# Up projection of a ConvFFN by seven block products instead of eight, with w_down and a gate by blocks of tokens

## The chip, the cores and the metric

One core of a Trainium2 chip. The metric is the device time of one execution in microseconds. Matmuls run on TensorE (PE), whose weight loads are shown as PEld; elementwise work on VectorE (DVE), ScalarE (ACT) and GpSimd (POOL); DMAs are issued from SyncE (SP).

## The reference

One inference step of a one-layer encoder over 1152 tokens (1024 of a prompt, 8 x 16 of samples), model width 1024, all in float32. The mixers (sparse attention, gated DeltaNet) and their merge come first, then what the change touches:

```python
x = x + mix @ w_out
h2 = rmsnorm(x, norm_ffn)
u_gate, u_val = split(h2 @ w_up, [D_FF], axis=-1)          # 1024 -> 2 x 2816
ext_f = concat([ffn_buf, u_gate], axis=1)
act = gelu(causal_dwconv(ext_f, conv_ffn), approximate=True)   # width 3
x = x + (act * u_val) @ w_down                             # 2816 -> 1024
gate_p = sigmoid(rmsnorm(x, norm_ple) @ w_ple_gate)        # 1024 -> 1024
x = x + gate_p * (p @ w_ple)
y = rmsnorm(x, norm_final)
```

## The kernel before, in words

Activations lie transposed: 128 features on the partitions, tokens along the free dimension. A dense product is a list of jobs (`_Job`, L245), each one weight tile of up to 8 x 128 rows and 128 output features. `weights` (L294) loads the tile ("wr"), casts it on ACT to a rounded part "wh" and subtracts on POOL (on DVE for jobs marked `late`) to get the rest "wl"; two pairs of wh and wl exist, so a tile is made while the two before it are used. `dense` (L345) runs a job's matmuls: for each of three blocks of 384 tokens and each k, three products of 128 x 128 by 128 x 384 into one PSUM bank (wh x H, wh x L, wl x H, where H and L are the activations' rounded part and rest), and an `evac` generator takes the bank from there. Three banks go round.

The order of all instructions is fixed ahead by a planner (`_Driver`, L75): each piece of work is a generator that asks for an engine or an event, and the piece that can start first by a table of costs goes next; `pick` (L1792) chooses between DVE and POOL by which is free first in that plan. Each engine then works through its list in that order, and so does SP with the DMAs.

The stages after the mixers are in `merge_ffn` (L2499). w_out (8 jobs) is evacuated by `evac_res` (L2309): add the residual x, store it (x2T), and make H2 and L2 of x times the norm's weight; the sum of squares goes along, and `rms` (L2357) makes the row R2 of reciprocal roots from it, by small matmuls and a Newton iteration of 11 small DVE instructions. The up projection is 44 jobs (`job_gate`, `job_val`, L2178, L2182), gate and value tile of one f in turn. `evac_gate` (L2364) multiplies by R2 into "fe", convolves on DVE into "fc", applies the gelu on ACT and multiplies by R2 again on POOL; `evac_val` (L2416) multiplies with the value product and splits the result into aH and aL, which stay in SBUF. So the FFN runs in four parts of 6, 6, 5 and 5 f: after each part w_down's 8 jobs over that part's rows run for all tokens, and their result is added to the residual through DRAM (x2T, x3T). The embedding's gate (w_ple_gate) runs for blocks 0 and 1 with one set of weights and then, weights loaded again, for block 2; `evac_pg` (L2458) applies it and `final` (L2484) the last norm.

```python
                    nc.tensor.matmul(acc, wh[:, kw], H, start=k == 0, stop=False)
                    nc.tensor.matmul(acc, wh[:, kw], L, start=False, stop=False)
                    nc.tensor.matmul(acc, wl[:, kw], H, start=False, stop=k == j.nk - 1)
```

Of the kernel before, what the change touches and what calls it, by code (L numbers as in the profile page):

```python
# [19 lines left out]
T = 1152  # L20
# [26 lines left out]
class _Banks:  # L47
# [16 lines left out]
    def give(self, t, at):  # L64
        self.free.append((at, self.held.pop(id(t))[1]))

# [178 lines left out]
class _Job:  # L245

    def __init__(self, src, nk, rhs, evac, m=128, blocks=range(NB), need=None, pre=None, late=0,
                 lag=False, spans=None):
# [6 lines left out]
        self.spans = spans or [slice(b * BW, b * BW + BW) for b in range(NB)]  # L255


class _Kernel:
# [34 lines left out]

    def weights(self):  # L294
# [4 lines left out]
        def fetch(j):  # L299
            wp, n = (self.wp2, "wr2") if j.late == 2 else (self.wp, "wr")  # L300
            j.raw = wp.tile([128, 8, 128], F32, name=n, bufs=1)[:, :j.nw, :j.m]
            nc.sync.dma_start(j.raw if len(j.evacs) == 1 else j.raw.rearrange("p (d k) c -> p d k c", k=j.nk), j.src)
        while True:
# [6 lines left out]
            if j.raw is not None and not j.late:  # L310
                yield j.loaded
            else:
                if j.raw is None:
                    yield SP
                    fetch(j)
                yield DMA
            nxt = next((x for x in self.jobs[i:] if x.src is not None), None)
            if j.late and nxt is not None:
                yield SP
                fetch(nxt)  # L320
            if len(used) > 1:
                yield used[-2].done
            wh = self.wp.tile([128, 8, 128], F32R, name="wh")[:, :j.nw, :j.m]
            yield ACT
            nc.scalar.copy(wh, j.raw)
            wl = self.wp.tile([128, 8, 128], F32R, name="wl")[:, :j.nw, :j.m]
            if j.late:
                yield DVE
                nc.vector.tensor_sub(wl, j.raw, wh.bitcast(F32))
            else:  # L330
                for k in range(0, j.nw, 2):
                    kk = slice(k, min(j.nw, k + 2))
                    yield POOL
                    nc.gpsimd.tensor_sub(wl[:, kk], j.raw[:, kk], wh[:, kk].bitcast(F32))
            j.w = wh, wl
            used.append(j)
            self.drv.set(j.prepared)
# [7 lines left out]
    def dense(self, jobs):  # L345
# [3 lines left out]
        for j in jobs:  # L349
            units = [(b, i, 0, j.nk) for i in range(len(j.evacs)) for b in j.blocks]  # L350
            if j.lag:
                units = [(b, 0, 0, j.nk - 1) for b in j.blocks] + [(b, 0, j.nk - 1, j.nk) for b in j.blocks]
            for b, i, k0, k1 in units:
                cols = j.spans[b]
                if k0 == 0:
# [10 lines left out]
                for k in range(k0, k1):  # L366
# [7 lines left out]
                    nc.tensor.matmul(acc, wh[:, kw], H, start=k == 0, stop=False)  # L374
                    nc.tensor.matmul(acc, wh[:, kw], L, start=False, stop=False)
                    nc.tensor.matmul(acc, wl[:, kw], H, start=False, stop=k == j.nk - 1)
                if k1 == j.nk:
                    if (b, i, k0, k1) == units[-1]:
                        drv.set(j.done)
                    drv.set(j.full[b])  # L380
        for e in ends:
            yield e

# [10 lines left out]
    def build(self):  # L394
# [5 lines left out]
        self.evs = _Banks(self.pool(ctx, "ev"), [128, BW], "evo", 4)  # L400
        self.accs = _Banks(self.pool(ctx, "psm", space=PSUM), [128, 512], "acc", 3, cols=BW)
# [20 lines left out]
        self.x3T = dp.tile([3, 8, 128, T], F32, name="x3T")  # L422
# [20 lines left out]
    def mixers(self):  # L443
# [37 lines left out]
        with ExitStack() as st:  # L481
# [6 lines left out]
            with ExitStack() as s2:  # L488
# [3 lines left out]
                drv.spawn(self.dense(jobs + self.jpp + self.jb), 9)  # L492
# [1636 lines left out]
    def merge_jobs(self):  # L2129
# [15 lines left out]
        self.jo = [_Job(I["w_out"][d], KD, two("MH", "ML"), self.evac_res(d, 0), pre=self.pre_load(lambda d=d: xT[d]),  # L2145
# [5 lines left out]
        self.A, self.C = {}, {}  # L2151
        self.aev = {f: [_Event() for _ in range(NB)] for f in range(22)}
        self.cev = {f: _Event() for f in range(22)}
        self.jf, f0 = [], 0
        for part, nf in enumerate((6, 6, 5, 5)):
            fs = list(range(f0, f0 + nf))
            if part == 0:
                self.jf.append(self.job_gate(fs[0]))
            for f in fs[1:] + [None]:
                if f is not None:  # L2160
                    self.jf.append(self.job_gate(f))
                elif part < 3:
                    self.jf.append(self.job_gate(f0 + nf))
                self.jf.append(self.job_val((f if f is not None else f0 + nf) - 1))
            src = (lambda d: self.x2T[d], lambda d: self.x3T[0][d], lambda d: self.x3T[1][d],
                   lambda d: self.x3T[2][d])[part]
            for d in range(8):
                self.jf.append(_Job(I["w_down"][d][:, f0:f0 + nf], nf,
                                    lambda k, cols, f0=f0: (self.A[f0 + k][0][:, cols], self.A[f0 + k][1][:, cols]),
                                    self.evac_res(d, part + 1), pre=self.pre_load(lambda d=d, src=src: src(d)),  # L2170
                                    need=lambda b, k, f0=f0: self.aev[f0 + k][b]))
            f0 += nf
        self.jp = [_Job(I["w_ple_gate"][d], KD, two("H3", "L3"), self.evac_pg(d), blocks=blocks,
                        pre=self.pre_ple(d), need=lambda b, k: self.rev[4][k][b],
                        late=(1 + d % 2) * (blocks == (2,))) for blocks in ((0, 1), (2,)) for d in range(8)]
        self.add_jobs(self.jpp + self.jb + self.ja + self.jo + self.jf + self.jp)

    def job_gate(self, f):  # L2178
        return _Job(self.I["w_up"][f], KD, lambda k, cols: (self.H2[:, k, cols], self.L2[:, k, cols]),
                    self.evac_gate(f), need=lambda b, k: self.rev[0][k][b])  # L2180

    def job_val(self, f):  # L2182
        return _Job(self.I["w_up"][22 + f], KD, lambda k, cols: (self.H2[:, k, cols], self.L2[:, k, cols]),
                    self.evac_val(f))
# [124 lines left out]
    def evac_res(self, d, step):  # L2309

        nc, drv = self.nc, self.drv

        def go(b, cols, acc, x):
# [3 lines left out]
            drv.give(self.accs, acc)  # L2317
            yield SP
            nc.sync.dma_start((self.x2T if step in (0, 4) else self.x3T[step - 1])[d][:, cols], x)
            if step in (0, 4):  # L2320
                H, L = (self.H2, self.L2) if step == 0 else (self.H3, self.L3)
                g = self.nrm[:, 1 if step == 0 else 2, d:d + 1]
                yield ACT
                nc.scalar.activation(H[:, d, cols], x, AF.Copy, scale=g)
                yield DVE
                nc.vector.scalar_tensor_tensor(L[:, d, cols], x, g, H[:, d, cols].bitcast(F32),
# [328 lines left out]
```

## Time and profile before

| | us |
|---|---|
| median of 3 runs | 2183.92 (2183.42 to 2184.28) |
| the profiled execution | 2187.6 |
| its span, first to last instruction | 2185.8 |
| busy: PE | 2117.6 (97%) |
| busy: DVE | 1227.8 (56%) |
| busy: POOL | 907.9 (42%) |
| busy: ACT | 847.9 (39%) |

The mean granted clock of TensorE was 0.988 of 2.4 GHz. Times of the trace count from the span's start. All instructions carry the line of one helper (L178), so they are told apart by their tiles: "acc" is a PSUM bank of a dense product, "rp" one of a norm.

### The profile page before, as it was taken

The numbers are of one execution on the slowest core, as the hardware profiler recorded it, in microseconds if no ns is written. First come the engines' busy times: TensorE is split into PE (matmuls) and PEld (weight loads), VectorE is DVE, ScalarE is ACT, GpSimd is POOL, SyncE is SP. The second block draws the span as 40 slices with busy tenths as digits, with TensorE's granted clock in tenths as the row PEclk, the third lists the DMA queues.
The fourth block names the chain that finished last, engine by engine and source line by source line (L and its number), as shares of the span: only waits on it lengthen the run. The fifth ranks groups of instructions, "written<-read, shape, count | busy, mean of one in ns | idle before, by whom it ended". The sixth has DMA issues, their size and how long they took to land.

```text
span 2185.8 us, 35741 instructions
## 1 busy us (share of the span) xinstructions
PE 2117.6 (97%) x12618; PEld 2061.5 (94%) x12618; DVE 1227.8 (56%) x3166; ACT 847.9 (39%) x1697; POOL 907.9 (42%) x1174
## 2 busy tenths in 40 slices
PE   7999988989999999999999999999999999999997
PEld 6898987989999889999999999999999999999997
DVE  7268988888757787774343444314441343244547
ACT  5266666566535556665133211101110111112432
POOL 5344433433234444454365445324442443343651
PEclk9999999989999999999999999999999999999998
DMA  5444366676655755457764311452135215413646
GB/s 192 121 119 102 79 179 160 157 200 178 178 171 161 217 161 170 141 163 230 235 203 143 90 40 40 91 168 46 47 65 172 64 40 128 134 40 97 193 155 202
DMA packets 326210, 298.99 MB, mean 137 GB/s; under 512 B 118332, under 2 KB 294032, under 8 KB 325904
## 3 DMA queue, kind: packets, MB, share of 16 engines
q1 hardware_dynamic: 326032, 296.71, 47.6%
q8 instruction: 100, 1.64, 0.4%
q14 instruction: 78, 0.64, 0.1%
HBM read 203.55 MB, written 94.71 MB: 136 GB/s over the span
## 4 chain that ended last, share of the span: by engine, by line
PE 62%; DMA 3%; DVE 1%; SPq 1%; issue 0%; POOL 0%; ACT 0%; DVEq 0%; ACTq 0%
PE acc L178 54%; PE at L178 7%; DMA evo<-gates 1%; PE rp L178 1%; DMA pbT<-evo 1%; SPq L178 1%; DMA r<-gsc 0%; DMA obT<-sg 0%; DMA sg<-sgb 0%; DVE evo L178 0%; DVE z L178 0%; POOL wl L178 0%; DVE X L178 0%; POOL tg L178 0%; DMA x<-qkv 0%
## 5 line engine op out<-in xcount | busy, mean ns | idle before, releaser
L178 PE MATMUL acc<-H,wh 128*128 128x384 f32 (+1 forms) x2592 | 897.2, 346 | 10.9 <-ACT wh L178 5.4
L178 PE MATMUL acc<-H,wl 128*128 128x384 f32 (+1 forms) x2592 | 876.9, 338 | 1.6 <-POOL wl L178 1.6
L178 PE MATMUL acc<-L,wh 128*128 128x384 f32 (+1 forms) x2592 | 876.5, 338 | 1.8 <-POOL L L178 1.3
L178 POOL TENSOR_TENSOR wl<-wr,wh 128x256 fp32r<-128x256 f32 (+1 forms) x572 | 484.2, 872 | 754.3 <-ACT wh L178 726.7
L178 PEld LDWEIGHTS acc<-H,wh 128*128 128x128 f32 x2592 | 488.9, 189 | 21.0 <-ACT wh L178 6.5
L178 PEld LDWEIGHTS acc<-L,wh 128*128 128x128 f32 x2592 | 489.1, 189 | 7.2 <-POOL L L178 2.0
L178 PEld LDWEIGHTS acc<-H,wl 128*128 128x128 f32 x2592 | 488.2, 188 | 4.3 <-POOL wl L178 2.9
L178 ACT CAST wh<-wr 128x1024 fp32r<-128x1024 f32 (+3 forms) x167 | 159.3, 954 | 580.3 <-PE acc L178 493.6
L178 DVE TENSOR_TENSOR xs<-xs,acc 128x384 f32<-128x384 f32 x120 | 66.5, 554 | 231.5 <-PE acc L178 146.0
L178 PE MATMUL acc<-aL,wh 128*128 128x384 f32 x528 | 178.0, 337 | 0.0
L178 PE MATMUL acc<-aH,wl 128*128 128x384 f32 x528 | 178.0, 337 | 0.0
L178 PE MATMUL acc<-aH,wh 128*128 128x384 f32 x528 | 178.0, 337 | 0.0
L178 DVE TENSOR_TENSOR fe<-acc,R 128x384 f32<-128x384 f32 (+1 forms) x88 | 38.2, 456 | 195.7 <-PE acc L178 195.7
L178 ACT ACTIVATE ja<-SC,cola 128x768 bf16<-128x768 f32 (+2 forms) x93 | 96.7, 1039 | 34.8 <-DVE cola L178 25.3
L178 PEld LDWEIGHTS acc<-aH,wl 128*128 128x128 f32 x528 | 99.0, 187 | 0.0
L178 PEld LDWEIGHTS acc<-aH,wh 128*128 128x128 f32 x528 | 99.0, 187 | 0.0
L178 PEld LDWEIGHTS acc<-aL,wh 128*128 128x128 f32 x528 | 99.0, 187 | 0.0
L178 POOL TENSOR_TENSOR ssq<-ssq,sqs 128x384 f32<-128x384 f32 x62 | 64.4, 1041 | 80.3 <-ACT sqs L178 80.0
L178 DVE SCALAR_TENSOR_TENSOR fc<-fe,cwf,fc 128x1024 f32<-128x1024 f32 (+1 forms) x88 | 95.0, 1080 | 3.1
L178 POOL TENSOR_TENSOR fc<-fc,R 128x288 f32<-128x288 f32 x88 | 75.0, 883 | 41.1 <-ACT fc L178 41.1
L178 DVE TENSOR_TENSOR sqs<-fc,acc 128x384 f32<-128x384 f32 x66 | 36.3, 550 | 79.7 <-PE acc L178 79.7
L178 ACT CAST aH<-sqs 128x384 fp32r<-128x384 f32 x66 | 33.8, 512 | 121.8 <-DVE sqs L178 121.8
(370 smaller groups left out, 3270.6 us busy)
## 6 DMA issues: line engine op xcount, KB each, us to landing
wr<-in_w_in SPq DMA_DIRECT2D x48, 512.0 KB, 3.7
wr<-in_w_up SPq DMA_DIRECT2D x44, 512.0 KB, 3.6
x3T<-xs SPq DMA_DIRECT2D x72, 192.0 KB, 1.9
xs<-x3T SPq DMA_DIRECT2D x72, 192.0 KB, 2.6
gates<-evo SPq DMA_DIRECT2D x48, 192.0 KB, 2.2
x2T<-xs SPq DMA_DIRECT2D x48, 192.0 KB, 2.0
xs<-x2T SPq DMA_DIRECT2D x48, 192.0 KB, 3.5
wr<-in_w_ple_gate SPq DMA_DIRECT2D x16, 512.0 KB, 3.5
```

Source lines behind the costliest of these rows:

```text
L178: r = f(*a, **k)
```

## The change

**Up projection.** For one f, the gate's weight tile is (a1, a2) and the value's (b1, b2), each half 4 x 128 rows of k; the input is cut into k halves and, in each block of 384 tokens, into a first and a second half of 192. That is a 2 x 2 by 2 x 2 block product, done by seven products (`_Up`, Strassen's scheme in Winograd's form) of 4 x 128 rows with 576 tokens, each in two PSUM banks of 288 columns (`up_products`). The weight sides are a1, a2, four sums of halves (`up_sums`: S1 = b1 + b2, S2 = S1 - a1, S3 = a1 - b1, S4 = a2 - S2) and b2; the token sides are two halves of the input and four sums T (`evac_out`, which takes the place of `evac_res` after w_out, and `up_parts`, which splits them). `evac_up` puts the products together with seven additions on DVE, `up_inner` convolves (first tap on ACT), applies the gelu and multiplies; the product goes to DRAM (AT). It is no longer multiplied by the norm's R2 on the value side: `evac_down` does that after w_down.

**w_down and gate.** For each block of 384 tokens: w_down with k in parts of 8, 8 and 6 tiles that accumulate in the same banks, output tiles 0 to 3 and then 4 to 7, followed by the 8 gate tiles. Every weight tile is loaded and split once per block. `load_up` brings a block's activations from DRAM and splits them; the residual is read from x2T straight into the result's buffer, and x3T goes. PSUM: three double banks (`ups`) in the up projection, the same as six single ones after it.

```diff
+A1X, A2X, S2T2, S3T3, S1T1, B2T4, S4Y = range(7)
...
+    def up_sums(self):
+        nc, q = self.nc, {}
+        for j in self.ju:
+            yield j.loaded
+            a1, a2, b1, b2 = j.raw
+            for n, i in enumerate((S1T1, S2T2, S3T3, S4Y)):
+                yield self.ju[j.f - 1].prepared[i] if j.f else self.hev2 if n < 2 else self.fev
+                o = q[n] = (self.hp if n < 2 else self.fp).tile([128, 4, 128], F32, name="s%d" % n, bufs=1)
+                x, y = ((b1, b2), (q[0], a1), (a1, b1), (q.get(1), a2))[n]
+                e, w = self.pick(DVE, POOL)
+                yield e
+                (w.tensor_sub if n else w.tensor_add)(o, x, y)
...
+    def up_rest(self, j, i, wh, wl):
+        e, q = self.pick(DVE, POOL) if j.f else (DVE, self.nc.vector)
+        n = 4 if e == DVE else 2
+        for k in range(0, 4, n):
+            yield e
+            q.tensor_sub(wl[:, k:k + n], j.parts[i][:, k:k + n], wh[:, k:k + n].bitcast(F32))
...
+    def up_products(self, j):
+        for i in range(7):
+            yield j.prepared[i]
+            wh, wl = j.w[i]
+            bank[i] = yield self.ups
...
+            for u in range(2):
+                acc = bank[i][:, u, :288]
+                for k in range(4):
+                    evs, H, L = self.up_rhs(i, u, k)
...
+                    nc.tensor.matmul(acc, wh[:, k], H, start=k == 0, stop=False)
+                    nc.tensor.matmul(acc, wh[:, k], L, start=False, stop=False)
+                    nc.tensor.matmul(acc, wl[:, k], H, start=False, stop=k == 3)
...
+        for b in range(NB):
+            for ds in (range(4), range(4, 8)):
+                heads = {}
+                for k0, k1 in ((0, 8), (8, 16), (16, 22)):
+                    for d in ds:
+                        j = _Job(I["w_down"][d][:, k0:k1], k1 - k0, up(k0), self.evac_down(d), blocks=(b,),
+                                 pre=self.pre_down(d), late=True, head=heads.get(d), last=k1 == 22,
+                                 need=lambda b, k, k0=k0: self.aev[k0 + k][b])
...
             for d in range(8):
...
+                self.jd.append(_Job(I["w_ple_gate"][d], KD, lambda k, cols, b=b: [x[:, k] for x in self.H3[b]],
+                                    self.evac_pg(d), blocks=(b,), pre=self.pre_ple(d), late=True,
+                                    need=lambda b, k: self.gev[k][b]))
...
+    def up_parts(self, t):
...
+        for k in range(4):
+            for b in range(NB):
+                yield self.opev[k][b]
+                yield self.tpev[4 + k][b]
+            R, H, L = self.TR[t][:, k], self.TH[t][:, k], self.TL[t][:, k]
+            yield ACT
+            nc.scalar.copy(H, R)
+            yield DVE
+            nc.vector.tensor_sub(L, R, H.bitcast(F32))
...
+    def evac_up(self, j, bank):
...
+        yield j.full[A1X]
+        yield ACT
+        nc.scalar.copy(u1, bank[A1X][:, :, :288])
...
+        yield from add(A2X, u3, u1)
+        yield from add(S2T2, u2, u1)
+        for e in self.Re[0]:
+            yield e
+        g, R = parts(ext[:, 2:2 + T]), parts(self.R2)
+        yield DVE
+        nc.vector.tensor_mul(g[:, 0], own(u3), R[:, 0])
+        yield from add(S3T3, u3, u2)
+        v = yield self.vs
+        vx, vy = [parts(v)[:, z] for z in range(2)]
+        yield from add(S1T1, vy, own(u3), OP.subtract, False)
+        yield from add(S1T1, u2, u2, OP.subtract)
+        yield from add(B2T4, vx, own(u3))
+        yield from add(S4Y, u2, u2, OP.subtract)
...
+    def load_up(self, b, fs):
+        for f in fs:
+            yield self.part_done[b - 1, f] if b else self.ju[21].done[(A1X, S2T2, S3T3, S1T1)[f // 6]]
+            yield self.ast[f]
...
+            nc.sync.dma_start(a, self.AT[f][:, b * BW:b * BW + BW])
+            yield DMA
+            yield ACT
+            nc.scalar.copy(H, a)
+            yield DVE
+            nc.vector.tensor_sub(L, a, H.bitcast(F32))
```

## Rows read from the trace of the kernel before

**Rows 1.** The page: the span and TensorE's share of it.

```profile
span 2185.8 us, 35741 instructions
...
PE 2117.6 (97%) x12618; PEld 2061.5 (94%) x12618; DVE 1227.8 (56%) x3166; ACT 847.9 (39%) x1697; POOL 907.9 (42%) x1174
```

**Rows 2.** Chain of waits: start us, us, engine, tile, instructions.

```profile
1133.33 92.48 PE acc L178 x532
...
1243.12 819.58 PE acc L178 x4707
...
2179.15 3.15 DVE X L178 x6
```

**Rows 3.** Windows: stretch, busy us of PE, PEld, DVE, ACT, POOL, clock, DMA.

```profile
1243.20:2062.60 819.40, 819.40 (x4709) 819.40 (x4707) 307.50 (x469) 152.80 (x211) 336.39 (x397) 1.00 0.34 88
1300.00:1400.00 100.00, 100.00 (x578) 100.00 (x578) 42.75 (x65) 18.44 (x24) 45.73 (x52) 1.00 0.23 44
2135.00:2169.00 34.00, 34.00 (x202) 34.00 (x202) 31.94 (x70) 13.28 (x21) 6.11 (x6) 1.00 0.77 252
```

**Rows 4.** Timeline of PE in w_out: start us, us, instruction.

```profile
1184.57 0.34 PE L178 MATMUL acc<-MH,wh 128*128 128x384 f32 x1
...
1185.09 0.34 PE L178 MATMUL acc<-MH,wh 128*128 128x384 f32 x1
```

**Rows 5.** Timeline, all engines, attention: 272 columns.

```profile
870.62 0.28 PE L178 MATMUL at<-skL,sbH 128*128 128x272 f32 x1
870.62 0.19 PEld L178 LDWEIGHTS at<-skH,sbH 128*128 128x128 f32 x1
...
870.74 0.29 PE L178 MATMUL at<-skH,sbH 128*128 128x272 f32 x1
...
870.99 0.34 PE L178 MATMUL acc<-H,wh 128*128 128x384 f32 x1
```

**Rows 6.** Timeline of PE in the input projection: 448 columns.

```profile
62.28 0.37 PE L178 MATMUL acc<-L,wh 128*128 128x448 f32 x1
...
63.11 0.37 PE L178 MATMUL acc<-H,wl 128*128 128x448 f32 x1
```

**Rows 7.** Lines by form, 1240 to 2060 us, DVE: busy us, mean ns.

```profile
L178 DVE SCALAR_TENSOR_TENSOR fc<-fe,cwf,fc 128x1024 f32<-128x1024 f32 x44 | 72.4, 1645 | 1.6
L178 DVE TENSOR_TENSOR xs<-xs,acc 128x384 f32<-128x384 f32 x94 | 52.1, 554 | 184.0 <-PE acc L178 113.6 <-DMA xs<-x3T 47.5 <-DMA xs<-x2T 20.1
L178 DVE TENSOR_TENSOR aL<-sqs,aH 128x384 fp32r<-128x384 f32 x66 | 51.0, 773 | 33.4 <-ACT aH L178 33.4
...
L178 DVE SCALAR_TENSOR_TENSOR fc<-fe,cwf,fc 128x128 f32<-128x128 f32 x44 | 22.7, 515 | 1.6
```

**Rows 8.** Lines by form, 1240 to 2060 us, POOL and ACT.

```profile
L178 POOL TENSOR_TENSOR wl<-wr,wh 128x256 fp32r<-128x256 f32 x251 | 232.0, 952 | 442.4 <-ACT wh L178 440.0 <-DMA out_cf<-fe 2.4
...
L178 ACT ACTIVATE H<-xs,nrm 128x384 fp32r<-128x384 f32 x22 | 13.5, 616 | 23.2 <-DVE xs L178 23.1
```

**Rows 9.** Timeline of DVE, around the norm and in the up projection.

```profile
1232.91 0.16 DVE L178 SCALAR_TENSOR_TENSOR rs_a<-rs_a,rr_m 128x3 f32<-128x3 f32 x1
...
1341.59 0.55 DVE L178 TENSOR_TENSOR aL<-sqs,aH 128x384 fp32r<-128x384 f32 x1
...
1344.66 1.05 DVE L178 TENSOR_TENSOR aL<-sqs,aH 128x384 fp32r<-128x384 f32 x1 [0.58 <-ACT aH L178]
```

**Rows 10.** Lines, 2136 to 2169 us (gate, last block), DVE and ACT.

```profile
L178 DVE TENSOR_TENSOR wl<-wr,wh 128x1024 fp32r<-128x1024 f32 x6 | 7.3, 1218 | 0.1
L178 ACT CAST wh<-wr 128x1024 fp32r<-128x1024 f32 x6 | 6.3, 1045 | 2.2 <-PE acc L178 2.2
```

**Rows 11.** The page: DMA packets, and issues (KB each, us to landing).

```profile
DMA packets 326210, 298.99 MB, mean 137 GB/s; under 512 B 118332, under 2 KB 294032, under 8 KB 325904
...
x2T<-xs SPq DMA_DIRECT2D x48, 192.0 KB, 2.0
xs<-x2T SPq DMA_DIRECT2D x48, 192.0 KB, 3.5
```

More of the change, by code (lines that the diff above doesn't have):

```diff
@@ L255, in __init__ @@
         self.spans = spans or [slice(b * BW, b * BW + BW) for b in range(NB)]
+        self.head, self.last = head or self, last
+class _Up:
+    src = 0
+    def __init__(self, f):
+        self.f, self.w = f, [None] * 7
+        self.prepared, self.done, self.full, self.summed = [[_Event() for _ in range(7)] for _ in range(4)]
+        self.loaded, self.parts = _Event(), {}
+A1X, A2X, S2T2, S3T3, S1T1, B2T4, S4Y = range(7)
 class _Kernel:
@@ L291, in split, with pair, part @@
         (self.nc.vector if eng == DVE else self.nc.gpsimd).tensor_sub(L, x, H.bitcast(F32))
+    def pair(self, used, k, c, m, ev):
+        if len(used) > 1:
+            yield used[-2]
+        used.append(ev)
+        return [self.wp.tile([128, 8, 128], F32R, name=n)[:, :k, :m] for n in ("wh", "wl")]
+    def part(self, wh, wl, raw):
+        nc = self.nc
+        yield ACT
+        nc.scalar.copy(wh, raw)
+        n = raw.shape[1]
+        for k in range(0, n, 2):
+            kk = slice(k, min(n, k + 2))
+            yield POOL
+            nc.gpsimd.tensor_sub(wl[:, kk], raw[:, kk], wh[:, kk].bitcast(F32))
     def weights(self):
@@ L316, in weights @@
                 yield DMA
[L317 to L323, printed above, removed]
-            yield ACT
[L325 to L334, printed above, removed]
@@ new lines, in landed, with down_weights @@
+    def landed(self, j, t):
+        self.drv.cur.dma = t
+        yield DMA
+        self.drv.set(j.loaded)
+    def down_weights(self, j, used):
+        n = len(self.down)
+        if n > 2:
+            yield self.down[-3]
+        else:
+            yield used[n - 2] if n < 2 else self.ju[21].done[B2T4]
+        self.down.append(j.done)
+        if n % 3 == 2:
+            t = self.TH[3].rearrange("p a b c -> p (a b c)")
+            wh, wl = [t[:, z:z + j.nw * 128].rearrange("p (k m) -> p k m", m=128) for z in (0, 1024)]
+        else:
+            wh, wl = [self.wp.tile([128, 8, 128], F32R, name=x)[:, :j.nw] for x in ("wh", "wl")]
+        yield j.loaded
+        yield ACT
+        self.nc.scalar.copy(wh, j.raw)
+        self.drv.spawn(self.down_rest(j, wh, wl), 1)
@@ new lines, in merge_ffn @@
+            for i in (1, 2):
+                self.ups.views[i] = p.tile([128, 2, 512], F32, name="up%d" % i)
+                self.ups.free.append((0.0, i))
+            self.accs = _Views([x[:, i, :BW] for x in self.ups.views for i in range(2)])
+            self.accs.free = []
+            ends = drv.spawn(self.dense(self.jd), 9, self.ju[21].done[S4Y])
+            drv.spawn(self.down_loads(), 1)
+            for i in range(4):
+                drv.spawn(self.load_up(0, range(i, 22, 4)), 1)
```

548 lines of the change are left out of this document (384 added, 164 removed).

## The prediction

> **What bounds the kernel now.** I read the page first. The span is 2185.8 us and TensorE (PE) is busy for 97% of it [rows 1]; the profiled execution took 2187.6 us, 3.7 us over the median of the three runs, 2183.92. The sum below is one of differences within that execution, and I lay it against the median.
>
> Then the chain of waits. From 1133 us to 2170 us it is matmul upon matmul: 92.48 us of the output projection, some 17 us with the norm's small matmuls and a few waits among them, then 819.58 us without a break [rows 2]. The windows say the same of that stretch: PE busy for 819.40 of 819.40 us, clock 1.00 (2.4 GHz), DVE busy for 38%, POOL 41%, and the DMA at 88 GB/s [rows 3]. The reader should see that in the ConvFFN nothing but PE counts: work taken from other engines there is worth nothing, and a matmul column saved is worth its full time as long as the others keep up. So the sum needs the price of a column, and the rest is whether the others keep up.
>
> **Matmuls: the gain.** Before, the up projection is 44 weight tiles x 3 token blocks x 8 k x 3 products = 3168 matmuls of 384 columns. After, it is 22 x 7 products x 2 halves x 4 k x 3 = 3696 matmuls of 288 columns: 7/8 of the columns in 7/6 of the instructions. No row has 288 columns, so I take the nearest sizes. Matmuls of 384 columns start (1185.09 - 1184.57) / 3 = 0.1733 us apart [rows 4]; 578 in 100 us gives 0.1730 [rows 3]. Those of 272 columns, each with weights of its own, start (870.99 - 870.62) / 3 = 0.1233 us apart [rows 5]; those of 448, (63.11 - 62.28) / 4 = 0.2075 us [rows 6]. Per column this is 0.451, 0.453 and 0.463 ns: in proportion, with no fixed part that can be seen. Between 272 and 384, 288 columns come to 0.1304 us. The stage goes from 3168 x 0.1733 = 549.0 us to 3696 x 0.1304 = 482.0 us: **-67.0 us**. The ends are 3/4 of 0.1733 (480.4 us, -68.6) and 288/448 of 0.2075 (493.0 us, -56.0). w_down (1584 matmuls) and the embedding's gate (576) keep count and size.
>
> A rule speaks against this. In the window the weight loads are busy for all of the time, just as the matmuls are [rows 3], and one takes 0.19 us [rows 5], more than the 0.1733 us between two matmuls. By the Trainium skill, "Perfetto Trace Analysis", Identifying the Most-Contended Engine, TensorE's headroom is to be judged by the busy share of LDWEIGHTS and not of the matmuls; by that this stage would be full of loads, and 528 more of them would make it longer. The trace bears it out as little as it can: in [rows 5] loads of 0.19 us follow each other at the matmuls' 0.12 us, so loads overlap and their share isn't the bound at 288 columns. It stays a rival.
>
> **The start of the up projection.** The first product needs only the rows of the first four output tiles; the second needs the last tile's third block through DVE (0.55, [rows 7]), ACT (0.62, [rows 8]) and twice DVE (some 1 us), about 2.5 us with handoffs, under a first product of 24 x 0.1304 = 3.1 us. The tight one is the sixth, which starts at 15.6 us and needs the third set of T operands; its last k is read some 1.2 us later. By then DVE has to do: the rest of the last evacuation 2.5; 12 splits of 576 columns; 4 weight splits of 512; 5 additions and products of 576; the reciprocal root, 11 x 0.16 [rows 9]. DVE's price by size comes from 550 ns for 384 columns (shortest, [rows 9]) and 1218 ns for 1024 [rows 10]: 0.149 us + 1.044 ns per column, so 0.75 for 576 and 0.68 for 512. The sum is 2.5 + 9.0 + 2.7 + 3.75 + 1.8 = 19.8 us against 16.8: **+3 us**, between 0 (the order hides it) and 6 (a few of these wait for POOL, below). Behind such a wait only PE's next products are queued. The norm's small matmuls are 9 + 9 as before.
>
> **The up projection, steady.** One f takes PE 168 x 0.1304 = 21.9 us. DVE now has, per f: 7 additions from PSUM of 576 columns, 5.25; the products with R, 0.75 + 1.2; the convolution, 4 x 512 and 2 x 128 columns, 5.0 (the groups of 1024 and 128, 1645 and 515 ns [rows 7], give 1.26 ns per column and 1.0 for 512); two products of 576, 1.5; together 13.7 us. Four sums and seven splits of 512 columns go to DVE or POOL, whichever the planner thinks free: with six on DVE 4.1, so 17.8 us of 21.9; POOL's five cost some 1.9 each (two of 256 at 952 ns, [rows 8]), 9.5 us. POOL's product with R is gone. ACT has seven casts of 512 columns, a copy of 576, three taps and the gelu of 1152 each, 6500 columns in all, which at 1045 ns for 1024 [rows 10] is 7 to 8 us. So no engine is over PE's time, but DVE is at 81% where it was at 38%, and DVE and POOL get into each other's way: a split of 384 columns takes 0.55 us alone and 1.05 when POOL works at the same time [rows 9], 773 ns on average [rows 7]. With the mean factor of 1.4 on the two-input work in SBUF that the group means do not already hold (1.95 + 1.5 + 4.1 = 7.55), DVE comes to 20.8 us. The PSUM ring holds three products, so an evacuation may be two products (6.3 us) late before PE notices; weights are made two products ahead. I take **+2 us** for the stage, between 0 and the rival below.
>
> **w_down and gate by blocks.** Every weight tile is loaded, cast and split for one block of 24 matmuls (4.2 us) and no longer for three. The trace shows this already: in its last 34 us the gate runs so, with a cast of 1045 ns and a split of 1218 ns per tile [rows 10], DVE at 94%, DMA at 252 GB/s, and PE busy for 34.00 of 34.00 us [rows 3]. The new stage asks for less of each: per tile a split in two halves (1.4), an activation's split 0.92 x 0.55 and a third of an evacuation (0.55 + 0.55 + 0.62), 2.5 of 4.2 us of DVE; and in 124.8 us per block (720 matmuls) 24.8 MB, which is 15.7 of weights, 4.3 of activations and 4.7 of residual, embedding and output: 198 GB/s. At the change from w_down to the gate the last tile goes DVE 0.55, DVE 0.55, ACT 0.62, DVE 0.6 and four handoffs, about 3.2 us, under 7 k of the first gate tile, 21 x 0.1733 = 3.6 us. Three such places, 0 to 1.5 us each: **+2 us** in all, from 0 to 5.
>
> **At nothing.** The activations' trip through DRAM: f = 21 needs some 10 us for its inner part, 2.0 and 3.5 us for store and load [rows 11] and 1 us for the split, some 17 us; the first matmul on it comes 8 tiles, 33 us, after the stage ends. The loads on SP wait for stores of f that were done one f earlier; behind a late one stand only later loads of the same kind, with four weight tiles already fetched. The x3T traffic (144 transfers) goes. The tail (last DVE work at 2179.15 [rows 2]) is unchanged.
>
> **Sum:** -67.0 + 3 + 2 + 2 = -60, so 2183.9 - 60 = **2124 us** (2128 for a profiled execution).
>
> **Rivals.** (a) DVE with POOL becomes the bound of the up projection. If each of the shared operations waits as long as the worst row (1.05 / 0.55 = 1.9), DVE needs 5.25 + 5.0 + 7.55 x 1.9 = 24.6 us per f, 2.7 over PE's, x 22 = 59 us, and the gain is gone. With the mean factor, nothing is lost. The middle gives 2153. For it: 1.4 to 1.9 is not far, and the order is fixed ahead by a planner. Against it: at 94% of DVE PE didn't wait [rows 3]. By the Trainium skill, "SBUF — State Buffer", Who interferes with whom, the pair of ports is an exclusive lock, which is how 0.55 becomes 1.05. Chance 0.15.
> (b) Slower: the weights of w_down and gate, loaded three times, set the pace through the DMA. If the queues carry no more than the kernel's mean of 137 GB/s [rows 11], a block takes 24.8 MB / 137 = 181 us for 125, +56 x 3 = 168, 2292 us. It cancels the gain at 67 us over three blocks, that is from about 170 GB/s down. Against it: 252 GB/s held for 34 us without a gap [rows 3]. Chance 0.05.
> (c) The change buys no PE time, as a matmul's pace is set by its weight load: 3696 x 0.1733 = 640.5, +91.5, with the +7 about 2282. Against it: [rows 5]. Chance 0.03.
>
> **Numbers.** Forecast 0.75, (a) 0.15, (b) 0.05, (c) 0.03, no difference for another reason 0.02. Faster by over 0.2% (4.4 us, about what can be told from no change) is the forecast and (a): 0.90; same 0.02; slower 0.08. The range goes from the largest gain without a stall (2183.9 - 68.6, and 2 us of waits around the norm that could go, 2113) to the middle of (a), 2153; that leaves out some 2 in 10.
>
> **What would show it.** Right: matmuls of 288 columns 0.130 us apart; the up stage near 482 us with PE at 100%, DVE near 80%; each block of w_down and gate near 125 us; clock 1.00. Wrong: PE idle repeatedly before S or T products (weights or operands from DVE and POOL: a); waits of the cast for w_down's DMA (b); 0.17 us between matmuls of 288 columns (c).

## The result, and the profile after

The changed kernel takes 2161.07 us (median of four runs, 2153.31 to 2164.95) against 2183.73: ratio 0.9892, 95% interval [0.9863, 0.9921]. In a second series of five runs it took 2160.96 against 2182.02, 0.9899 [0.9881, 0.9917]. It is faster by 21 to 23 us, where 60 were forecast, and the forecast's range (2113 to 2153) doesn't hold it.

The profiled execution took 2153.31 us. It is the shortest run of the changed kernel, and that of the old kernel, 2187.6, one of its longest, so the two spans differ by 34.3 us and not by 22. The table, read from the starts of PE's matmuls, says where:

| stretch | before, us | after, us | difference |
|---|---|---|---|
| to the first w_out matmul | 1127.6 | 1113.5 | -14.0 |
| w_out | 104.1 | 102.7 | -1.4 |
| last w_out matmul to the last of the gate | 937.6 | 917.8 | -19.8 |
| of which up projection (288 columns) | | 506.5 | |
| of which w_down and gate | | 411.0 | |
| behind it | 16.5 | 17.5 | +1.0 |

The first row is not the change's (shown below), and the last isn't either: behind the last gate matmul the profiles of both kernels show 16.5 us in some runs and 17.5 in others. Nor can 1.4 us be told in w_out, which took 102.1 to 105.2 us over the profiles of kernels that leave nothing out. The third row is the change's: it repeats to 0.5 us in either kernel (937.6 again in e2_before_ev_right, 917.3 to 917.8 in the changed kernel's other two), and it was forecast as -60. The page of the profile after:

```profile
span 2151.5 us, 37608 instructions
PE 2065.3 (96%) x13146; PEld 2005.0 (93%) x13146; DVE 1543.1 (72%) x3585; ACT 1001.0 (47%) x1979; POOL 838.2 (39%) x1028
```

PE lost 52 us of busy time against [rows 1], and DVE gained 315. The windows of the profile after, by stage (columns as in [rows 3]): the first block f = 0 of the up projection, the blocks after it, and w_down with the gate.

```profile
1216.40:1255.10 38.70, 32.57 (x205) 31.27 (x205) 27.48 (x46) 15.41 (x28) 13.37 (x13) 0.87 0.22 61
1255.10:1700.00 444.90, 444.90 (x3357) 444.90 (x3356) 366.67 (x470) 148.38 (x241) 255.53 (x249) 1.00 0.39 75
1723.00:2134.00 411.00, 391.24 (x2221) 382.53 (x2220) 262.58 (x477) 168.61 (x251) 45.17 (x41) 1.00 0.57 173
```

The middle line is what [rows 3] showed of the old kernel: PE never idle, clock 1.00, though DVE is now at 82%. The losses stand in the other two: 6 us idle and a granted clock of 0.87 in the first block, 20 us idle in the last stage. There the waits of PE are (us in total, times, longest):

```profile
PE up L192 <- DVE gt L192: 12.0, 15, 1.4
PE up L192 <- ACT wh L192: 3.0, 4, 0.7
PE up L192 <- ACT T3H L192: 2.2, 3, 0.7
PE up L192 <- DVE L L192: 1.4, 3, 0.6
PE up L192 <- DVE T2L L192: 0.9, 1, 0.9
PE up L192 <- ACT H L192: 0.2, 1, 0.2
```

`gt` is the tile into which DVE evacuates an accumulator. That is odd, for six accumulators go round and PE needs one every 4.2 us. The timeline of one such place, in the gate (start us, us; in brackets the engine's idle time and what ended it):

```profile
1836.50 0.34 PE L192 MATMUL up<-H,T3H 128*128 128x384 f32 x1
1836.67 0.34 PE L192 MATMUL up<-H,wh 128*128 128x384 f32 x1
...
1838.90 1.01 DVE L192 TENSOR_TENSOR gt<-up,R 128x384 f32<-128x384 f32 x2
...
1840.28 0.34 PE L192 MATMUL up<-H,wl 128*128 128x384 f32 x1
1840.66 0.56 DVE L192 TENSOR_TENSOR gt<-up,R 128x384 f32<-128x384 f32 x1 [0.75 <-PE up L192]
...
1841.27 0.44 PE L192 MATMUL up<-H,wh 128*128 128x384 f32 x1 [0.65 <-DVE gt L192]
1841.56 0.33 PE L192 MATMUL up<-L,wh 128*128 128x384 f32 x1
```

An output of the gate is 24 matmuls. The third ends with the matmul of 1836.50 (weights in `T3H`), the fourth begins at 1836.67 (weights in `wh`) and goes into another PSUM bank. DVE evacuates the first two outputs from 1838.90 on. Then it stands idle for 0.75 us before it takes the third, which has long been complete: it starts only when the fourth output's 18th matmul, of 1840.28, is over. And PE goes on with the 19th only when DVE is done, 0.99 us after the 18th instead of 0.17. So each engine waits for the other, though the two are at different banks. Every second output of the gate has this (1841.27, 1849.50, 1857.73), and two in four of w_down's third parts: 21 of the 26 pauses of over 0.6 us from start to start. The waits put down to ACT's weight copies are of this kind too, but for the first: at 1763.34, 1812.20 and four more places PE goes on 0.15 us after an evacuation's end. All that lies over the usual distance of the matmuls in this stage comes to 27.8 us.

### The profile page after: what moved, and what is told of

It is laid out like the page before. It is cut to its first block, busy times and chain, and to the rows that moved or that the text cites. A ratio compares the mean times of both kernels' runs of the same rounds, so it can differ in the third digit from the quotient of the medians.

```text
span 2151.5 us, 37608 instructions
## 1 busy us (share of the span) xinstructions
PE 2065.3 (96%) x13146; PEld 2005.0 (93%) x13146; DVE 1543.1 (72%) x3585; ACT 1001.0 (47%) x1979; POOL 838.2 (39%) x1028
## 4 chain that ended last, share of the span: by engine, by line
PE 56%; DVE 4%; DMA 4%; issue 1%; ACT 1%; POOL 1%; SPq 1%; DVEq 0%; ACTq 0%; POOLq 0%
PE up L192 38%; PE acc L192 12%; PE at L192 6%; PE rp L192 1%; SPq L192 1%; DVE B L192 1%; DVE gt L192 1%; DVE wl L192 1%; DMA evo<-gates 1%; DMA T<-in_w_down 0%; POOL tg L192 0%; POOL wl L192 0%; DVE z L192 0%; DMA obT<-sg 0%; DMA x<-qkv 0%
## 5 line engine op out<-in xcount | busy, mean ns | idle before, releaser
L192 PE MATMUL acc<-H,wh 128*128 128x384 f32 (+2 forms) x1344 | 475.6, 354 | 6.9 <-DVE evo L192 2.1
L192 PE MATMUL acc<-L,wh 128*128 128x384 f32 (+2 forms) x1344 | 456.6, 340 | 1.8 <-POOL L L192 1.3
L192 PE MATMUL acc<-H,wl 128*128 128x384 f32 (+2 forms) x1344 | 456.6, 340 | 1.4 <-POOL wl L192 1.4
L192 POOL TENSOR_TENSOR wl<-wr,wh 128x256 fp32r<-128x256 f32 (+1 forms) x288 | 232.5, 830 | 302.0 <-ACT wh L192 285.8
L192 PEld LDWEIGHTS acc<-H,wh 128*128 128x128 f32 (+1 forms) x1344 | 253.5, 189 | 15.8 <-DVE evo L192 2.4
L192 PEld LDWEIGHTS acc<-L,wh 128*128 128x128 f32 (+1 forms) x1344 | 253.8, 189 | 6.9 <-POOL L L192 2.0
L192 PEld LDWEIGHTS acc<-H,wl 128*128 128x128 f32 (+1 forms) x1344 | 253.4, 189 | 3.6 <-POOL wl L192 2.4
L192 PE MATMUL up<-B,wh 128*128 128x288 f32 x704 | 143.2, 297 | 3.5 <-DVE B L192 2.8
L192 DVE SCALAR_TENSOR_TENSOR T<-fe,cwf,T 128x512 f32<-128x512 f32 x132 | 124.6, 944 | 17.8 <-ACT T L192 16.4
L192 PE MATMUL up<-T,wh 128*128 128x288 f32 (+1 forms) x416 | 125.6, 302 | 2.2 <-DVE T L192 2.2
```

The lines of the kernel that those rows point to most:

```text
L192: r = f(*a, **k)
```

## The experiments

Times of stages are from each kernel's profile: "first block" from the first matmul of f = 0 to that of f = 1, "up" and "w_down, gate" from first to last matmul. The median is of all timed runs (one run where marked *).

| kernel | first w_out matmul | first block | up | w_down, gate | median |
|---|---|---|---|---|---|
| changed | 1113.5 | 38.7 | 506.5 | 411.0 | 2161.07 |
| changed, again (c_after_again) | 1117.8 | 38.7 | 506.5 | 410.5 | 2160.96 |
| e3_after_ev_left | 1121.0 | 38.7 | 506.4 | 410.9 | 2158.30 |
| e1_ring | 1120.0 | 38.7 | 506.4 | 394.7 | 2139.64 |
| e1b_ring_again | 1118.5 | 35.6 | 503.3 | 394.6 | 2139.67 |
| e10_six_tiles | 1113.9 | 38.7 | 506.4 | 392.3 | 2138.13 |
| e9_gate_pair | 1118.1 | 37.0 | 504.8 | 391.1 | 2137.95 |
| e6_256 (256 columns) | 1114.1 | 38.7 | 484.3 | 391.0 | 2111.53* |
| e4_ring_late_parts | 1119.7 | 40.0 | 507.7 | 395.2 | 2142.42 |
| e5_casts_first | 1126.0 | 40.5 | 508.2 | 392.6 | 2150.44* |
| e7_no_norm | 1113.2 | 36.3 | 504.5 | 395.1 | 2133.43* |
| e8_no_low | 1123.6 | 27.0 | 496.0 | 393.7 | 2133.12* |

### The pauses in w_down and the gate

The six accumulators are the two halves of three two-bank tiles, and successive outputs got half a and half b of the same tile. **e1_ring** changes their order alone (`_Ring` hands them out in strict rotation):

```diff
-self.accs = _Views([x[:, i, :BW] for x in self.ups.views for i in range(2)])
+self.accs = _Ring([x[:, i, :BW] for i in range(2) for x in self.ups.views])
...
-self.accs.free += [(self.drv.cur.t, i), (self.drv.cur.t, i + 1)]
+self.accs.free += [(self.drv.cur.t, i), (self.drv.cur.t, i + 3)]
```

> The changed kernel with another order of its six accumulators in w_down and the gate: successive outputs get halves of different two-bank tiles instead of the two halves of one. Every engine keeps its instructions and their order. Theory A (a matmul into one half of a tile waits for VectorE's read of the other half, and lets go about 0.15 us after that read ends): nearly all of the 26 pauses of about 1 us, 27.8 us together, go; from the first to the last matmul of w_down and the gate 411.0 us becomes 384 to 388, and the whole 20 to 27 us less. Theory B (the matmul waits for an accumulator that is really still in use, or for its weights): the pauses stay where they are, 411 us, and the whole changes by less than 3 us.

Measured: 394.7 us for the stage, 16.3 less, and a median of 2139.64 (0.9796 [0.9768, 0.9825] of the old kernel). That is short of theory A's 384 to 388, as nearly all was expected to go. Of the 21 pauses at an evacuation none stays where it was; but 11 pauses of over 0.6 us are there, and counted as the 27.8 us were, 11.7 us are left (the expectation of e9 counts 9 pauses with 9.7 us, by a narrower measure). The other five of the 26 stay, and six are new. Two of the six are of the old kind, at the gate's fourth output, which gets the other half of the tile of the first, and the first waits for the norm:

```profile
PE up L204 <- DVE gt L204: 1.4, 2, 0.7
```

But this moves two things at once: which tile an output belongs to, and which bank DVE reads while PE writes. **e10_six_tiles** parts them. It keeps the order and the banks, and closes the up projection's PSUM pools to declare six tiles of one bank each:

```diff
+for st, side, of in ((self.up1, None, (1, 2)), (self.up0, "right", (0,))):
+    if got >= set(of):
...
+        st.close()
+        p = self.pool(st, "dn%d" % of[0], space=PSUM, **({"side": side} if side else {}))
+        for i in range(2 * of[0], 2 * of[-1] + 2):
+            self.accs.views[i] = p.tile([128, 512], F32, name="dn%d" % i)[:, :BW]
...
```

> The changed kernel with its accumulators in the old order, successive outputs in neighbouring PSUM banks as before, but each bank declared as a tile of its own once the up projection is done with it. Instructions, order and banks stay; what can differ is only which waits the program's own bookkeeping puts on the matmuls. Theory A (the 1 us pauses are that bookkeeping's: a read of one half of a tile holds up writes to the other half): the pauses go as they did with the other order, w_down and the gate take 393 to 397 us instead of 411. Theory B (the chip itself holds a matmul back while VectorE reads the neighbouring bank): 409 to 412 us, and only another order of banks helps.

Measured: 392.3 us, 18.7 less than the changed kernel and just below theory A's 393; median 2138.13 (0.9822 [0.9797, 0.9846]). Its window and the waits of PE in it:

```profile
1723.40:2115.70 392.30, 386.90 (x2221) 383.46 (x2220) 262.08 (x477) 167.75 (x251) 49.73 (x41) 1.00 0.59 181
```

```profile
PE rp L192 <- POOL ssq L192: 1.5, 2, 0.8
PE dn L192 <- DVE L L192: 1.5, 3, 0.6
PE dn L192 <- ACT H L192: 1.1, 3, 0.6
PE dn L192 <- DVE T2L L192: 0.9, 1, 0.9
PE dn L192 <- ACT T3H L192: 0.3, 1, 0.3
```

Every engine has the instructions of the changed kernel in the same order (DVE 262 us in both windows), but no wait for `gt` is left, and one of 0.3 us for a weight copy. The place in the gate that answers to the one above, on PE, in the middle of the fourth output, and on DVE, which evacuates the first three outputs in one go:

```profile
1836.91 0.34 PE L192 MATMUL dn<-H,wl 128*128 128x384 f32 x1
1837.09 0.34 PE L192 MATMUL dn<-H,wh 128*128 128x384 f32 x1
1837.26 0.34 PE L192 MATMUL dn<-L,wh 128*128 128x384 f32 x1
1837.43 0.34 PE L192 MATMUL dn<-H,wl 128*128 128x384 f32 x1
```

```profile
1836.04 1.48 DVE L192 TENSOR_TENSOR gt<-dn,R 128x384 f32<-128x384 f32 x3
```

DVE reads the third output's bank to 1837.52 without having waited, and PE goes on in the neighbouring one at 0.173 us a matmul. (That the banks are those of the changed kernel follows from the edit; the profile doesn't number them.) So the chip doesn't hold the matmul back: the wait was in the program. Its bookkeeping of who reads and writes what goes by tiles: a read of half a had to wait for the writes to half b that stood ahead of it, and held up the next write to half b. (By the Trainium skill, "PSUM — Partial Sum Buffer", PSUM bank collisions raise a hardware error, a matmul's write and another engine's read at the same time raise an error in one bank and run clean in two different ones; the rows, with two banks, agree.)

**e9_gate_pair** goes for the pauses that are left. It is e1_ring with the gate's first two outputs of each block taken together, k = 0 to 6 of both, then k = 7 of both:

```diff
+for k0, k1 in ((0, 7), (7, 8)):
+    for j in (j0, j1):
...
+        for k in range(k0, k1):
+            yield j.need(b, k)
```

> As the kernel with the new order of accumulators; in each block of tokens the first two outputs of the gate take seven of their eight k first, both of them, and then the last k of both, so that TensorE has 3.6 us more work before it needs what w_down's last output leaves. Theory A (the pauses that are left in this stage, 9 of them with 9.7 us, are the three handovers from w_down to the gate: the last k waits for the last output's high and low part, 1.7 us, then the norm's matmul for GpSimd's sum, 1.1 us, and the third accumulator for an evacuation that waits for the norm, 1.1 us): 4 to 8 us of them go, 394.8 becomes 387 to 391. Theory B (the chain behind w_down's last output is longer than this cover, or the waits only move to the norm): 393 to 396.

Measured: 391.1 us, 3.6 less; 7.9 of the 11.7 us are left. The waits for w_down's last output are gone, and one of the two for the norm's sum; those for an evacuation behind the norm went from two with 1.4 us to three with 2.2. That is just short of theory A's 387 to 391; in the median (2137.95 against 2139.67) it can't be told.

### The start of the up projection

In the first block PE waits 6.1 us, and behind the waits the clock is low. The timeline of the changed kernel, DVE and POOL at the end of w_out (1216.2 us), then PE:

```profile
1214.70 0.41 DVE L192 SCALAR_TENSOR_TENSOR T<-xs,nrm,sqs 128x192 f32<-128x192 f32 x1
1217.30 1.08 DVE L192 TENSOR_TENSOR T2L<-T,T2H 128x576 fp32r<-128x576 f32 x1 [2.19 <-ACT T2H L192]
1218.30 1.46 DVE L192 SCALAR_TENSOR_TENSOR T<-xs,nrm,T 128x192 f32<-128x192 f32 x1
...
1221.09 2.11 DVE L192 TENSOR_TENSOR wl<-s,wh 128x512 fp32r<-128x512 f32 x2
...
1224.12 0.60 DVE L192 SCALAR_TENSOR_TENSOR B<-xs,nrm,B 128x384 fp32r<-128x384 f32 x1
```

```profile
1217.73 1.82 POOL L192 TENSOR_TENSOR s<-s,wr 128x512 f32<-128x512 f32 x1
```

```profile
1224.77 0.40 PE L192 MATMUL up<-B,wh 128*128 128x288 f32 x1 [2.83 <-DVE B L192]
...
1228.22 0.44 PE L192 MATMUL up<-T1H,wl 128*128 128x288 f32 x1
1228.46 0.44 PE L192 MATMUL up<-T1H,wh 128*128 128x288 f32 x1
```

Splits of T2 and of weights stand on DVE ahead of the last evacuation of w_out, whose last piece of B2 comes at 1224.12, eight microseconds after its matmul. **e4_ring_late_parts** (e1_ring with one line, ahead of all the splits) puts that right:

```diff
 def up_parts(self, t):
...
+    yield self.opev[7][NB - 1]
```

> As the kernel with the new order of accumulators, and the splits of the transposed sums T2, T1 and T4 into two parts (ScalarE copy, VectorE subtraction) wait until the last evacuation of w_out is done. Theory A (the start of the up projection is lost because the last evacuation stands on VectorE behind those splits, PE then waits 0.9 and 3.1 us and TensorE's granted clock falls behind the waits): both waits fall to under 1 us together, the half-speed stretch at the second and third product goes, and the first block's seven products take 32 to 35 us instead of 38.7; the whole 4 to 7 us less than with the order of accumulators alone. Theory B (there is as much VectorE work ahead of the products either way): the waits move to the fourth to sixth product, whose operands are now split later, and the whole stays within 2 us.

Measured: 40.0 us, no gain, so theory A is out. The wait for B2 is gone, and 6.0 us of waits for T2, T1 and T4 are there. **e5_casts_first** reorders two queues (all copies of these operands first; T2's subtractions behind the last evacuation) and gives T4's subtractions to GpSimd:

```diff
-nc.scalar.copy(H, R)
-yield DVE
-nc.vector.tensor_sub(L, R, H.bitcast(F32))
+nc.scalar.copy(self.TH[t][:, k], self.TR[t][:, k])
+if t == 2:
+    yield self.opev[7][NB - 1]
...
+e, w = (POOL, nc.gpsimd) if t == 3 else (DVE, nc.vector)
+for k in range(4):
+    yield e
+    w.tensor_sub(self.TL[t][:, k], self.TR[t][:, k], self.TH[t][:, k].bitcast(F32))
```

> As the kernel with the new order of accumulators; of the transposed sums T2, T1 and T4 all ScalarE copies are issued first, ahead of the weight copies of the later products, T2's VectorE subtractions wait for the last evacuation of w_out, and T4's subtractions go to GpSimd. Theory A (the start is lost in the order of two queues: on VectorE the last evacuation stands behind splits, on ScalarE the copies of T1 and T4 stand behind weight copies that wait for TensorE): the first block's seven products take 28 to 32 us instead of 38.7, and fewer slices show half clock. Theory B (VectorE has too much work at the start, 28 us in the first 40, whatever the order): 36 to 40 us stay, the waits only move, as they did when the splits were merely put later.

Measured: 40.5 us, theory B's side (36 to 40); DVE is busy for 30.5 us of it, and 2.6 us of waits now name GpSimd. **e7_no_norm** takes the norm away:

```diff
-pt = yield self.rpb
-yield PE
-for i in range(9):
-    nc.tensor.matmul(pt[:, i:i + 1], self.ssq[:, i * 128:i * 128 + 128], self.ones[:, 0:1],
...
+nc.vector.memset(self.R2, 1.0)
```

> As the kernel with the new order of accumulators, without the norm ahead of the up projection: the sums of squares are not reduced over partitions, no reciprocal root is taken, and the scale R is set to 1. That takes the 36 small TensorE matmuls (4.3 us with the pauses around them) and some 15 small VectorE operations out of the first block. Theory A (this serial chain on TensorE and VectorE makes the waits and the half clock of the second half of the first block): 38.7 us becomes 30 to 32.5, more than its own 4.3 us. Theory B (it costs its own time only, and the waits for T1 and T4 stay): 34 to 35 us.

Measured: 36.3 us. That is 2.4 us less, not even the norm's own 4.3 us: PE's waits went up from 6.1 to 9.5 us, the longest 4.5 for T1. Neither theory's figure, and a difference that one program shows between two runs (last section). With the norm gone PE comes sooner to operands that are no earlier. **e8_no_low** takes away the suspected work itself:

```diff
-yield DVE
-nc.vector.tensor_sub(L, R, H.bitcast(F32))
...
-return self.tev[t][k], self.TH[t][:, k, u], self.TL[t][:, k, u]
+return self.tev[t][k], self.TH[t][:, k, u], (self.TL if t == 1 else self.TH)[t][:, k, u]
```

> As the kernel with the new order of accumulators, without the low parts of the transposed sums T2, T1 and T4: their twelve VectorE subtractions of 576 columns are left out, and the matmuls that read a low part read the high part again. TensorE keeps all its matmuls, ScalarE its copies, the norm stays. Theory A (the start waits for VectorE, which has these 12 x 0.75 us = 9 us and more, stretched while GpSimd runs, ahead of the fourth to sixth product): the first block takes 25 to 30 us instead of 38.7. Theory B (the waits come from the copies on ScalarE that stand behind weight copies, or from the norm): 35 us or more.

Measured: 27.0 us, theory A. The window of its first block, and the one wait of PE in it:

```profile
1224.70:1251.70 27.00, 26.62 (x205) 26.38 (x205) 17.79 (x33) 15.04 (x28) 13.84 (x14) 1.00 0.30 87
```

```profile
PE up L204 <- DVE B L204: 0.4, 1, 0.4
```

DVE falls from 27.5 to 17.8 us, the waits from 6.1 to 0.4, the clock rises from 0.87 to 1.00, and what is left over the 22.3 us of a later block is the norm. So twelve subtractions with some 9 us set the start; an order that helps one of them makes another late.

### The price of a product's columns

**e6_256** (e1_ring, `acc = bank[i][:, u, :256]` from the second block on):

> As the kernel with the new order of accumulators, with 256 of the 288 columns in every product from the second block on (the other 32 columns of each product are left out). It measures what a narrower product costs. Theory A (time goes with the columns, by the line through the old kernel's 272 and 384 columns, 0.449 ns a column, and the 2.2 ns that the 288 columns lie above that line are a constant of these operands): 0.116 to 0.119 us between matmuls, 19.5 to 20 us for a block's 168 matmuls. Theory B (a floor near 0.13 us, as each matmul loads its own weights): 0.130 to 0.133 us, 22 us a block, as with 288 columns.

Measured: 0.118 us between matmuls where PE doesn't wait, theory A: 1.8 ns above the line, where 288 columns lie 2.1 above it. But a block takes 21.2 us on average, not 19.8: in ten places, some 42 us or two blocks apart, PE waits for the low part of a weight tile, nine times 1.8 us and once 3.6, and behind five of the ten it runs at half clock. The waits in 440 us of it:

```profile
PE up L204 <- DVE wl L204: 19.4, 10, 3.6
```

At the first of them ACT's copy of the tile ends at 1305.41, and DVE's split of it starts at 1311.65, behind other DVE work without a gap; its matmul follows at 1312.38. So DVE's queue ahead of such a split is what comes next under the up projection, a few per cent below its present time.

### The 14 us ahead of w_out

Up to w_out the two kernels have the same instructions in the same order on every engine; buffers lie elsewhere, as the evo buffers went to the other side of SBUF. **e2_before_ev_right** does that alone in the old kernel, **e3_after_ev_left** undoes it in the changed one:

```diff
 # e2_before_ev_right
-self.evs = _Banks(self.pool(ctx, "ev"), [128, BW], "evo", 4)
+self.evs = _Banks(self.pool(ctx, "ev", side="right"), [128, BW], "evo", 4)
 # e3_after_ev_left
-self.evs = _Banks(self.pool(self.evst, "ev", side="right"), [128, BW], "evo", 4)
+self.evs = _Banks(self.pool(ctx, "ev"), [128, BW], "evo", 4)
-self.xs = _Banks(self.rp, [128, BW], "xs", 4)
+self.xs = self.evs
```

> The old kernel with one word changed: its evo buffers lie on the other side of SBUF, where the changed kernel has them, so that the mixers' buffers lie at the changed kernel's addresses. Theory A (addresses): the first w_out matmul starts near 1113.6 us instead of 1127.6, and the whole falls from 2183.7 to about 2170. Theory B (chance, or something that only the changed kernel does): 1127.6 and 2183 to 2185 stay, as in the old kernel's own runs, which lie within 0.9 us.

> The changed kernel with its evo buffers put back on the side of SBUF where the old kernel had them (from w_out on they serve as the xs buffers, for want of room), so that the buffers of the mixers lie at the old addresses. Theory A (the 14.0 us that the mixers won, which no instruction of theirs accounts for, come from where the buffers lie): the first w_out matmul starts near 1127.6 us again instead of 1113.6, and the whole is 11 to 14 us more than the changed kernel. Theory B (the mixers' time differs from run to run, whatever the addresses): the first w_out matmul starts anywhere between 1113 and 1128, and the whole stays in the changed kernel's 2153 to 2165 us.

Measured: the old kernel with the new addresses takes 2182.88 us, 1.0003 [0.9989, 1.0018]; its profile starts w_out at 1117.1 us, neither theory's figure. The changed kernel with the old addresses starts w_out at 1121.0 and takes 2158.30, inside its usual runs. So addresses don't explain the 14 us. The repeats say the rest:

> The changed kernel itself again. Theory A (its stages from w_out on repeat to a tenth of a microsecond, and its runs differ in the mixers alone): 506.4 us for the up projection and 411 us for w_down and the gate, the first w_out matmul anywhere from 1113 to 1128 us, the whole 20 to 24 us under the old kernel. Theory B (the 14 us that the mixers won in its first profile are the change's): the first w_out matmul near 1113.5 us again, the whole 30 us or more under the old kernel.

> The kernel with the new order of accumulators once more, beside the changed kernel and on the same chip. Theory A (the order of accumulators takes 16 us off w_down and the gate, and the rest of the differences between whole runs is the mixers' own, 1113 to 1128 us in the profiles so far): the median lies 13 to 20 us under the changed kernel's, w_down and the gate at 394 to 396 us again, the up projection at 506.4. Theory B (part of the 21 us between the medians so far belonged to the order too): 20 us or more.

Measured: the changed kernel starts w_out at 1117.8, e1_ring at 1120.0 and 1118.5, e10_six_tiles at 1113.9, though up to there their instructions are the same. The start moves between 1113 and 1128 us from run to run. The old kernel's own runs, within 0.9 us of each other in the first series, spread from 2175.19 to 2187.93 in later ones. In e1b the order is worth 21.3 us against the changed kernel's median, past theory A's 13 to 20 and just inside theory B's: 16 of the stage, 3 of the first block (below) in the profiles, the rest ahead of w_out. What in the mixers moves is spread out: matmul by matmul, the old kernel's profile is 5 us behind the changed kernel's at 185 us, 9 at 350, 12.6 at 500 and 14.0 at 700. One of the places: in the old kernel's profile ACT waits at 181.95 us for a transfer of `qr`, and PE 1.96 us behind it; in the changed kernel's PE waits for nothing there.

```profile
181.95 0.51 ACT L178 CAST qs<-qr 128x384 fp32r<-128x384 f32 x1 [3.07 <-DMA qr<-qiT]
...
183.19 0.47 PE L178 MATMUL ix<-kH,qs 128*128 128x512 f32 x1 [1.96 <-DVE qs L178]
```

Which transfers vary, and why, stays open.

## Why the prediction was wrong, step by step

The forecast's steps against the stretch behind w_out, 937.6 to 917.8 us:

| step | forecast | measured | off by |
|---|---|---|---|
| matmuls of the up projection | 482.0 | 3696 x 0.1326 = 490.1 | +8 |
| start | +3 (0 to 6) | 38.7 - 22.3 - 4.3 of the norm = 12.1 | +9 |
| up projection, steady | +2 | 0 | -2 |
| w_down and gate | +2 (0 to 5) | 27.8 of pauses | +26 |

Together +41, and the forecast missed this stretch by 60 - 19.8 = 40.2.

- **"w_down and gate by blocks"** failed, and it was most of the miss. The step priced engines (DVE 2.5 of 4.2 us, DMA 198 GB/s) and neither became the limit: DVE was busy for 262.6 of 411 us, 2.9 per tile, and 181 GB/s were moved in the 392.3 us of e10_six_tiles. It put the sharing of accumulators at nothing without a reason, as the description of the change takes the three double banks for "the same as six single ones". They are six views of three tiles. Its proof, the old gate's 34.00 of 34.00 us [rows 3], couldn't show that, as there each accumulator is a tile of its own ("acc", one bank). 16.3 us of the stage went with another order, 18.7 with other tiles. The handovers from w_down to the gate, the only loss that the step named, cost some 7.5 of the 11.7 us that e1_ring left, and not 2: besides the last output's parts the norm's sum waits there, and 1.8 us of them are the shared tiles again.
- **"The start of the up projection"** was right in part and too small: there is too much DVE work ahead of the T products, "19.8 us against 16.8", and e8_no_low shows it. But 3.4 of the 6.1 us of waits stood at the second product, which the step had called covered: it took the last evacuation to go first on DVE, and splits stood ahead of it. Missing, too, was what lateness brings with it. Waits of 0.6 and 2.8 us were followed by matmuls 0.24 us apart instead of 0.13, so PE pays twice; such matmuls are most of what the waits leave of the 12.1 us. And DVE's work ran beside GpSimd's sums of weights, which the step had in its upper bound alone: 1.46 us at 1218.30 for an operation that took 0.41 at 1214.70, while GpSimd was adding from 1217.73 to 1219.55.
- **The price of 288 columns** was mis-sized by 2.2 ns: 0.1326 us on 3490 pairs of matmuls, not 0.1304. "In proportion, with no fixed part that can be seen" came from three or four starts of each size. The old trace has 62 pairs of 272 columns without a wait (0.119 to 0.132 us), with a median of 0.125, from which the same line gives 0.132.
- **Rival (a)**, DVE as the bound, stayed out: PE busy for 444.90 of 444.90 us. At 256 columns it appears. **Rival (b)**: no wait for a weight transfer is among PE's waits, and the stage ran on 181 GB/s. **Rival (c)**: matmuls of 288 columns are 0.133 us apart, with the loads busy for all of the time. The pace went with the columns, 0.118 us at 256. The Trainium skill's rule ("Perfetto Trace Analysis", Identifying the Most-Contended Engine) would have had the loads' busy share as the bound; the runs don't bear that out.
- **"At nothing"**: the trip through DRAM cost PE at most one wait, 0.9 us for an activation's split (`T2L` above). The tail is as it was (16.5 or 17.5 us). That the mixers vary by 14 us between runs was not in the range at all.

The signs named for a right forecast did tell: blocks of w_down and gate of 136.5 to 138.0 us instead of 125 point at the step that failed, before any experiment.

## What to carry to other kernels

When a change makes one buffer serve as several (halves of a tile, views of a ring), ask what the program's bookkeeping takes as its unit: here reuse went by the tile, in both directions, and giving successive outputs different tiles, or each bank a tile of its own, was worth 16 to 19 us with not one instruction changed. A stage that begins with many operands to prepare should be summed by what is due at each product, with the slower clock behind each wait in the price. And time a kernel's stages in several profiles before a difference of spans is given to the change.

The best that was run is the changed kernel with the accumulators' order or tiles mended: 2138 to 2140 us, 0.980 to 0.982 of the old kernel. The two repairs of the last stage, six tiles and paired gate outputs, were not run together. For the start no repair was found.

## What the runs showed that I had not expected

- Many short pauses cost no clock in one stage, a few longer ones did in another. In w_down and the gate 26 pauses, none with over 1.4 us of idle time, left the granted clock at 1.00 (the third window above). Behind 0.6 and 2.8 us of waiting at the second product it fell to half, 1.2 GHz, came back, fell again at 1232.3 though PE had not waited since 1224.77, and once more behind waits of 0.5 and 1.8 us. Two windows of the changed kernel, the first two of these stretches:

```profile
1225.00:1229.00 4.00, 4.00 (x20) 4.00 (x20) 2.41 (x5) 1.93 (x4) 0.58 (x1) 0.57 0.02 4
1233.00:1235.50 2.50, 2.50 (x12) 2.50 (x12) 0.84 (x3) 0.00 (x0) 1.72 (x2) 0.50 0.46 95
```

- It isn't the same each time. In e6_256 four of nine equal waits of 1.8 us were followed by half clock and five were not. One program, e1_ring, with the same waits to a tenth of a microsecond in its first block (2.8, 2.2, 0.6, 0.5 us), had that block once in 38.7 us and once in 35.6:

```profile
1223.30:1262.00 38.70, 32.53 (x206) 31.24 (x206) 27.49 (x46) 15.42 (x28) 13.38 (x13) 0.87 0.23 61
```

```profile
1222.70:1258.20 35.50, 29.37 (x205) 28.07 (x205) 27.51 (x46) 15.44 (x28) 13.39 (x13) 0.95 0.25 66
```

So differences of 1 to 3 us in the first block, as those of e4, e5, e7 and e9, say little by themselves; the 11.7 us of e8 do.

- Where PE doesn't wait, a block's time repeats: 22.280 us on average over the blocks from the sixth on, in every kernel with all 288 columns that kept its splits and its norm.
